# Residual sums of the post norms: from loaded tiles on VectorE and GpSimd to accumulating transfers into the scaled tile

## The chip, the cores and the metric

The kernel runs on one core of a Trainium2 chip. Its engines are named as in the profile: PE (TensorE, the matrix engine, with PEld for its weight loads), DVE (VectorE), ACT (ScalarE), POOL (GpSimd) and SP (SyncE, which here issues most transfers). Every engine works through its own list of instructions strictly in order, and engines wait for each other through semaphores. The metric is the device time of one execution in microseconds (us).

## The reference

One layer of a decoder over 1024 prompt tokens and 64 sample tokens (8 sequences of 8), model width 1024, all in fp32:

```
x = x + 1/2 * post1(SwiGLU_1(pre1(x)))          # FFN1, inner width 2816
h = pre_mix(x); z = h @ w_in + b_in
    A: sliding-window attention (window 128), 8 heads, 2 KV heads, sinks
    B: HGRN2 gated linear recurrence, chunkwise, 4 heads of 128 x 128
x = x + post_mix(concat(norm(attn), gate(hgrn)) @ w_out)
x = x + 1/2 * post2(SwiGLU_2(pre2(x)))          # FFN2

def rms_norm(x, g):
    y = x * rsqrt(mean(x * x, -1) + 1e-6)
    return y * g
```

So three times a branch's output y is multiplied by a factor per token (the inverse root) and a gain per feature, and added to the residual x. This sum, `x + scaled y`, is what the change touches. It is then both the input of the next norm and, stored to a buffer, the residual of the sum after it; after FFN2 it is the output.

## The kernel before

**Tiling.** The 1088 tokens form three thirds. Third 0 has 320 tokens (256 of the prompt and the 64 sample tokens) and is kept feature-major: a tile is 128 features by 320 tokens, eight of them make the width, and they lie in two `big` tiles of 128 x 4 x 384. Thirds 1 and 2 have 384 tokens each and are token-major where the norms run: two `big` tiles of 128 x 3 x 512, one for each half of the width (`hf`), with three blocks of 128 tokens (`i`). fp32 matmuls are made of three passes with operands split in a high and a low part (`mm3`, L260 to L262, after a cast on ACT, L240, and a subtraction on DVE, L241), so each weight tile must pass ACT and DVE before PE can use it. Thirds 1 and 2 share their FFN matmuls as seven products of sums and differences, the units p1 to p7 of `f.pair`.

**Stages.** FFN1 for third 0, then the units of thirds 1 and 2; w_in, mixer and w_out by thirds, mixed with the last units of FFN1 and the first of FFN2; FFN2; output. A norm runs as a *stream*: a generator that `stream(name, ...)` starts and that moves one `yield` further at certain points between groups of matmuls (`tick`), until `need(name)` runs it to its end. The streams give the program its order; a scheduler then lists the instructions of each engine from its own simulated timeline, so that the final order can differ from the program's.

**Post norms.** `post_t` (L335) is the feature-major form. After the broadcast of the inverse root, which `bcast_steps` makes from squares on ACT (L318, L321), it goes through the eight feature tiles: load 160 KB of the residual to a tile `xt` on SP (L346), scale the branch's tile by gain and root on DVE (L347), add `xt` on POOL (L349); at the end the sum is stored. It is used three times: after FFN1 (residual x0, stream c0), after the mixer (residual x1T, stream c0 again) and at the end (residual x2T, to the output of the sample and the first part of the prompt). `post_n` (L412) is the token-major form: for each of three blocks of tokens it loads two `xt` tiles of 256 KB (L416) and makes scale and sum in one DVE instruction (L428), six in all; where a destination `xdst` is given, each is stored at once (L430). It is used five times: after FFN1 for thirds 1 and 2 (streams c1, c2, residual in_x_rest), after the mixer for thirds 1 and 2 (residual x1N) and at the end for third 1 (residual x2N, stored to the output). Third 2's last sum has code of its own.

**What follows a post norm.** `pre_t`, `pre_n` and `pre_s` make the next norm of the sum. For thirds 1 and 2, `row_rms` takes squares on ACT (L383) and, behind each pair of squares, stores the sum as the next residual from ACT's queue (x1N, x2N, L388); after the root on DVE (L389 and on) both halves are scaled (L447/L449, L503) and PE transposes them (`tr`, L457, L513) for the following matmuls. `raw` is the staging tile of weight loads; L986 loads the differences of weights that FFN2's units use from a buffer `fb`.

Of the kernel before, what the change touches and what calls it, by code (L numbers as in the profile page):

```python
# [13 lines left out]
AF = mybir.ActivationFunctionType  # L14
ALU = mybir.AluOpType
# [3 lines left out]
P = 128  # L19
# [15 lines left out]
C_F1POST, C_MPRE, C_MPOST, C_F2PRE, C_F2POST, C_BIN, C_LB, C_HGN, C_AON = (  # L35
    0, 8, 16, 24, 32, 40, 62, 70, 71)
# [11 lines left out]
def tile_step(ctx: ExitStack, tc: tile.TileContext, A: dict, O: list):  # L48
    nc = tc.nc
    V, S, G, PE = nc.vector, nc.scalar, nc.gpsimd, nc.tensor  # L50
# [48 lines left out]
    def stream(name, gen, rate):  # L99
        streams[name] = [gen, rate, 0.0]  # L100
# [28 lines left out]
    cols = cp.tile([P, NROWS], F32, name="cols")  # L129
    f1pre = cp.tile([P, KC], F32, name="f1pre")  # L130
    halfpost = cp.tile([P, 16], F32, name="halfpost")
# [155 lines left out]
    def tmp2(name, shape=(P, 512)):  # L287
        return pp.tile(list(shape), F32, tag="t2", bufs=8, name=uid(name))
# [46 lines left out]
    def post_t(y, xsrc, gpost, xdst=None):  # L335

        w = WIDTH[0]

        def part(d):
            return y[d // 4][:, d % 4, :w]  # L340

        rb = []
        yield from bcast_steps(part, w, rb)
        for d in range(KC):
            xt = tmp2("xt")
            nc.sync.dma_start(xt[:, :w], xsrc(d))  # L346
            V.scalar_tensor_tensor(part(d), part(d), gpost[:, d:d + 1], rb[0],  # L347
                                   op0=ALU.mult, op1=ALU.mult)
            G.tensor_tensor(part(d), part(d), xt[:, :w], op=ALU.add)  # L349
            if d % 2:  # L350
                yield
        if xdst is not None:
            for hf in range(2):
                nc.sync.dma_start(xdst[:, 4 * hf:4 * hf + 4], y[hf][:, :, :w])

    def pre_t(y, gpre, h):
        w = WIDTH[0]

        def part(d):
            return y[d // 4][:, d % 4, :w]  # L360

        rb = []
        yield from bcast_steps(part, w, rb)
        h[0] = new_h(0)
        for d in range(KC):
            t = tmp2("ht")
            V.scalar_tensor_tensor(t[:, :w], part(d), gpre[:, d:d + 1], rb[0],
                                   op0=ALU.mult, op1=ALU.mult)
            hi, lo = hcol(h[0], d, w)
            split(hi, lo, t[:, :w], G)  # L370
            if d % 2:
                yield
# [37 lines left out]
            yield  # L410

    def post_n(n, y, sm, xsrc, xdst=None):  # L412
        def load(i):
            t = [tmp2("xt") for _ in range(2)]
            for hf in range(2):
                nc.sync.dma_start(t[hf], xsrc[i * P:(i + 1) * P, hf * 512:hf * 512 + 512])  # L416
            return t

        xt = load(0)
        V.scalar_tensor_tensor(sm[:, 0, 0:3], sm[:, 0, 0:3], EPS, sm[:, 0, 4:7], op0=ALU.add, op1=ALU.add)  # L420
        rsqrt(sm[:, 1, 0:3], sm[:, 0, 0:3], (sm[:, 2, 0:3], sm[:, 3, 0:3]))
        for i in range(3):
            if i:
                xt = load(i)
            for hf in range(2):
                cs = slice(hf * 512, hf * 512 + 512)
                t = y[hf][:, i]
                V.scalar_tensor_tensor(t, t, sm[:, 1, i:i + 1], xt[hf], op0=ALU.mult, op1=ALU.add)  # L428
                if xdst is not None:
                    nc.sync.dma_start(xdst[i * P:(i + 1) * P, cs], t)  # L430
            yield

    def pre_n(n, y, gpre, h, dst):

# [105 lines left out]
    x1T = dr.tile([P, KC, WIDTH[0]], F32, name="x1T")  # L540
    x2T = dr.tile([P, KC, WIDTH[0]], F32, name="x2T")
# [9 lines left out]
    def x0_part(d, n=1):  # L551
        return A["x0T"][:, d * WIDTH[0]:(d + n) * WIDTH[0]].rearrange("p (k t) -> p k t", k=n)
# [120 lines left out]
            wts.fill()  # L673
        return rb, banks

    def x0_all(d):
        return x0_part(d)[:, 0]

# [994 lines left out]
    def seq(*gens):  # L1675
        for g_ in gens:
            yield from g_

    RM = [0.88, 1.08, 1.24]
    RA0, RA1, RB0, RB1 = 1.2, 0.75, 0.6, 0.8  # L1680
# [15 lines left out]
    part = {}  # L1696
# [3 lines left out]
    hmix, hffn2 = {}, {}  # L1700
# [12 lines left out]
    def done1(n):  # L1713
        y, g = f1.ys[n], cols[:, C_MPRE:C_MPRE + 8]
        if n == 0:
            stream("c0", seq(post_t(y, x0_all, halfpost[:, 0:8], x1T), pre_t(y, g, hmix)), RA0)
        else:
            need("half")
            stream(f"c{n}", seq(half_n(y, 2 - n, sums[n], A["norm_ffn1_post"], 0.5),
                                post_n(n, y, sums[n], xN[n - 1]), pre_n(n, y, g, hmix, x1N[n - 1])), RA1)  # L1720
# [27 lines left out]
    part = {}  # L1748

    def done_mix(n):  # L1750
        y, g = ym[n], cols[:, C_F2PRE:C_F2PRE + 8]
        if n == 0:
            stream("c0", seq(post_t(y, lambda d: x1T[:, d], cols[:, C_MPOST:C_MPOST + 8], x2T), pre_t(y, g, hffn2)), RB0)
        else:
            stream(f"c{n}", seq(post_n(n, y, sums[n], x1N[n - 1]),
                                pre_s(n, y, g, part, f2.SF, x2N[n - 1])), RB1)
# [31 lines left out]
        w_out_units(2, ym, sums)  # L1788
        done_mix(2)
    def out0():  # L1790
        yield from post_t(f2.ys[0], lambda d: x2T[:, d], halfpost[:, 8:16], O[1])

    tail = {}

# [120 lines left out]
```

## Time and profile before

| | |
|---|---|
| time, median of 3 runs | 1937.84 us (1935.99 to 1938.87) |
| profiled execution: span from first to last instruction | 1937.4 us |
| PE busy | 1923.1 us (99%) |
| DVE / ACT / POOL busy | 1430.7 (74%) / 946.0 (49%) / 186.1 (10%) us |
| mean granted clock of PE | 0.999 |
| data moved by DMA | 375.56 MB, mean 194 GB/s |
| transfers on the queues q1 and q10 (kind: hardware_dynamic) | 169680 and 5904 packets, 56.0% and 1.5% of the engines' span |

The profile was taken from an execution of its own; its span is given, and the times of the three runs stand beside it. An engine that is busy for 74% of the span may be waiting for nothing and nobody may wait for it: what counts is which wait of PE it ends. In a group's row stand line, engine, operation, output<-input, count, and durations in ns (least/median/most). All transfers of this kernel are issued from SP or ACT; POOL issues none.

### The profile page before, as it was taken

How to read it: one execution, taken by the hardware profiler on the slowest of the kernel's cores; microseconds unless marked ns; L12 is line 12 of the kernel's file. 1: busy time of each engine (PE TensorE's matmuls, PEld its weight loads, DVE VectorE, ACT ScalarE, POOL GpSimd, SP SyncE). 2: the span in 40 equal slices, each digit the busy share in tenths (PEclk: the TensorE clock that was granted, in tenths of full speed). 3: DMA queues.
4: the chain of work that ended last, by engine and by line, in shares of the span. 5: the costliest groups of instructions: out<-in, count | busy, mean ns of one | idle time of the engine just before them, and what ended most of it. 6: DMA issues, size and time to landing. Idle time of an engine off the chain costs nothing.

```text
span 1937.4 us, 34843 instructions
## 1 busy us (share of the span) xinstructions
PE 1923.1 (99%) x13547; PEld 1806.1 (93%) x13547; DVE 1430.7 (74%) x2469; ACT 946.0 (49%) x1701; POOL 186.1 (10%) x227
## 2 busy tenths in 40 slices
PE   9999999999999999999999999999999999999998
PEld 9999999999998987788999888989999999999886
DVE  6896789877568666787678758756987887656666
ACT  5553444444455434545445545846544444445452
POOL 0300000000004022020221212000000000000102
PEclk9999999999999999999999999999999999999999
DMA  6643676555767556765334344546555555667974
GB/s 248 209 133 115 232 267 247 206 191 184 242 217 242 180 155 215 283 220 163 114 102 153 99 140 142 164 147 209 185 198 192 198 188 189 210 228 241 308 255 141
DMA packets 175750, 375.56 MB, mean 194 GB/s; under 512 B 16144, under 2 KB 67536, under 8 KB 175568
## 3 DMA queue, kind: packets, MB, share of 16 engines
q1 hardware_dynamic: 169680, 362.84, 56.0%
q10 hardware_dynamic: 5904, 10.49, 1.5%
q8 instruction: 106, 1.74, 0.4%
q14 instruction: 60, 0.49, 0.1%
HBM read 290.86 MB, written 83.39 MB: 193 GB/s over the span
## 4 chain that ended last, share of the span: by engine, by line
PE 88%; DMA 6%; DVE 3%; ACT 1%; issue 1%; POOL 1%; SPq 0%; ACTq 0%; DVEq 0%; POOLq 0%
PE mm L260 27%; PE mm L262 26%; PE mm L261 26%; DMA ar<-fa 1%; DMA xt<-in_x_rest_dram 1%; DMA ar<-act 1%; PE lv L1337 1%; PE sc L1237 1%; DMA raw<-in_ffn_w_gu_dram 1%; PE pv L1283 1%; DVE w L241 1%; PE pT L1269 1%; PE c L262 0%; PE c L260 0%; PE c L261 0%
## 5 line engine op out<-in xcount | busy, mean ns | idle before, releaser
L260 PE MATMUL mm<-h,wsph 128*128 128x320 f32 (+1 forms) x1344 | 427.2, 319 | 0.4 <-DVE big L814 0.4
L261 PE MATMUL mm<-h,wsph 128*128 128x320 f32 (+1 forms) x1344 | 425.5, 317 | 0.2 <-DVE h L241 0.2
L262 PE MATMUL mm<-h,wspl 128*128 128x320 f32 (+1 forms) x1344 | 422.6, 316 | 0.0
L241 DVE TENSOR_TENSOR wspl<-raw,wsph 128x1024 fp32r<-128x1024 f32 x208 | 260.8, 1255 | 125.2 <-ACT wsph L240 124.1
L240 ACT CAST wsph<-raw 128x1024 fp32r<-128x1024 f32 x208 | 217.8, 1049 | 254.0 <-PE mm L261 199.3
L260 PEld LDWEIGHTS mm<-h,wsph 128*128 128x128 f32 x1344 | 252.2, 188 | 4.2 <-issue 2.3
L261 PEld LDWEIGHTS mm<-h,wsph 128*128 128x128 f32 x1344 | 252.5, 188 | 3.9 <-issue 2.3
L262 PEld LDWEIGHTS mm<-h,wspl 128*128 128x128 f32 x1344 | 251.9, 188 | 3.4 <-issue 3.1
L240 ACT CAST w<-raw 128x512 fp32r<-128x512 f32 (+1 forms) x208 | 153.8, 745 | 199.9 <-PE mm L261 96.2
L261 PE MATMUL mm<-h,w 128*128 128x384 f32 (+1 forms) x736 | 245.6, 334 | 0.3 <-DVE h L622 0.3
L260 PE MATMUL mm<-h,w 128*128 128x384 f32 (+1 forms) x736 | 245.7, 334 | 0.2 <-ACT h L620 0.2
L262 PE MATMUL mm<-h,w 128*128 128x384 f32 (+1 forms) x736 | 239.6, 333 | 0.5 <-POOL w L613 0.4
L241 DVE TENSOR_TENSOR w<-raw,w 128x512 fp32r<-128x512 f32 (+1 forms) x208 | 178.3, 861 | 72.6 <-ACT w L240 71.7
L261 PE MATMUL mm<-w,h 128*128 128x512 f32 x462 | 180.5, 391 | 0.7 <-DVE w L241 0.7
L260 PE MATMUL mm<-w,h 128*128 128x512 f32 x462 | 180.8, 394 | 0.0
L262 PE MATMUL mm<-w,h 128*128 128x512 f32 x462 | 179.8, 391 | 0.0
L260 PE MATMUL mm<-big,w 128*128 128x384 f32 x528 | 176.7, 335 | 0.3 <-ACT big L806 0.2
L261 PE MATMUL mm<-big,w 128*128 128x384 f32 x528 | 176.5, 334 | 0.0
L262 PE MATMUL mm<-big,w 128*128 128x384 f32 x528 | 176.0, 334 | 0.0
L261 PEld LDWEIGHTS mm<-h,w 128*128 128x128 f32 x736 | 138.1, 188 | 1.1 <-DVE h L622 0.8
L260 PEld LDWEIGHTS mm<-h,w 128*128 128x128 f32 x736 | 138.1, 188 | 0.8 <-ACT h L620 0.5
L262 PEld LDWEIGHTS mm<-h,w 128*128 128x128 f32 x736 | 137.6, 188 | 1.0 <-POOL w L613 0.7
(367 smaller groups left out, 3353.8 us busy)
## 6 DMA issues: line engine op xcount, KB each, us to landing
raw<-in_ffn_w_gu_dram SPq DMA_DIRECT2D x162, 512.0 KB
raw<-in_ffn_w_down_dram SPq DMA_DIRECT2D x74, 512.0 KB
raw<-in_w_in_dram SPq DMA_DIRECT2D x54, 512.0 KB
ar<-fa SPq DMA_DIRECT2D x70, 384.0 KB
big<-in_ffn_w_down_dram SPq DMA_DIRECT2D x88, 256.0 KB
fb<-big SPq DMA_DIRECT2D x44, 512.0 KB
fa<-big SPq DMA_DIRECT2D x22, 768.0 KB
raw<-fb SPq DMA_DIRECT2D x30, 512.0 KB
```

Source lines behind the costliest of these rows:

```text
L240: made['S'] = S.copy(hi, src).ins
L241: (lo_eng or V).tensor_tensor(lo, src, hi.bitcast(F32), op=ALU.subtract)
L260: PE.matmul(out, a[0], b[0], start=first, stop=False, skip_group_check=resume)
L261: PE.matmul(out, a[0], b[1], start=False, stop=False, skip_group_check=resume)
L262: return PE.matmul(out, a[1], b[0], start=False, stop=last, skip_group_check=resume).ins
L1237: PE.matmul(banks[g][rows(hq), i, cs], zq[rows(g), 2 * pr + i, b * P + 64 * hq:b * P + 64 * hq + 64], kx[rows(g), k0 + cs.start:k0 + cs.st ...
L1269: PE.transpose(tb2[hq][:, g, i, slot], pt[g][rows(hq), c:c + P], ident[rows(hq), rows(hq)])
L1283: PE.matmul(ob[par][rows(g), :, hq], vn[rows(par), b + (blk + hq) // 2, rows(g)], pT[hq][rows(par), g, :, PLACE[hq][blk]], start=alone or ...
L1337: PE.matmul(b5[32 * i:32 * i + 32, b, a], K[:, a, cs], Q[:, a, cs], start=True, stop=True)
```

## The change

In `post_t` the loaded tile and POOL's addition are gone. DVE scales as before; behind each second feature tile GpSimd issues a transfer that reads two feature tiles of the residual (128 x 2 x 320, 320 KB) from memory and adds them to the scaled tile in place (`accum_op=ALU.add`): four for each use. One `yield` more follows.

In `post_n` the loads and the six DVE instructions are gone. The first half of the width (`hf` 0) is scaled by three DVE instructions, the second by three of ACT, and behind each half GpSimd issues one accumulating transfer of 768 KB (128 x 3 x 512). The store to `xdst`, where there is one, is one of 768 KB for each half instead of three of 256 KB. The work goes half by half instead of block by block, and yields stand after the root, after each half and at the end.

In all 24 additions on POOL, 30 sums on DVE and 54 loads on SP go, and 15 scalings on DVE, 15 on ACT and 22 accumulating transfers on POOL's queue come: 12 of 320 KB and 10 of 768 KB. The lines behind the change are numbered 3 lower than before.

```diff
@@ -342,13 +342,13 @@
         rb = []
         yield from bcast_steps(part, w, rb)
         for d in range(KC):
-            xt = tmp2("xt")
-            nc.sync.dma_start(xt[:, :w], xsrc(d))
             V.scalar_tensor_tensor(part(d), part(d), gpost[:, d:d + 1], rb[0],
                                    op0=ALU.mult, op1=ALU.mult)
-            G.tensor_tensor(part(d), part(d), xt[:, :w], op=ALU.add)
+            if d % 2:
+                nc.gpsimd.dma_start(y[d // 4][:, d % 4 - 1:d % 4 + 1, :w], xsrc(d - 1), accum_op=ALU.add)
             if d % 2:
                 yield
+        yield
         if xdst is not None:
             for hf in range(2):
                 nc.sync.dma_start(xdst[:, 4 * hf:4 * hf + 4], y[hf][:, :, :w])
@@ -410,25 +410,22 @@
             yield
 
     def post_n(n, y, sm, xsrc, xdst=None):
-        def load(i):
-            t = [tmp2("xt") for _ in range(2)]
-            for hf in range(2):
-                nc.sync.dma_start(t[hf], xsrc[i * P:(i + 1) * P, hf * 512:hf * 512 + 512])
-            return t
-
-        xt = load(0)
         V.scalar_tensor_tensor(sm[:, 0, 0:3], sm[:, 0, 0:3], EPS, sm[:, 0, 4:7], op0=ALU.add, op1=ALU.add)
         rsqrt(sm[:, 1, 0:3], sm[:, 0, 0:3], (sm[:, 2, 0:3], sm[:, 3, 0:3]))
-        for i in range(3):
-            if i:
-                xt = load(i)
-            for hf in range(2):
-                cs = slice(hf * 512, hf * 512 + 512)
+        yield
+        for hf in range(2):
+            cs = slice(hf * 512, hf * 512 + 512)
+            for i in range(3):
                 t = y[hf][:, i]
-                V.scalar_tensor_tensor(t, t, sm[:, 1, i:i + 1], xt[hf], op0=ALU.mult, op1=ALU.add)
-                if xdst is not None:
-                    nc.sync.dma_start(xdst[i * P:(i + 1) * P, cs], t)
-            yield
+                if hf:
+                    S.activation(t, t, AF.Copy, scale=sm[:, 1, i:i + 1])
+                else:
+                    V.tensor_scalar(t, t, sm[:, 1, i:i + 1], None, op0=ALU.mult)
+            nc.gpsimd.dma_start(y[hf], xsrc[0:384, cs].rearrange("(i p) c -> p i c", p=P), accum_op=ALU.add)
+            yield
+            if xdst is not None:
+                nc.sync.dma_start(xdst[0:384, cs].rearrange("(i p) c -> p i c", p=P), y[hf])
+        yield
 
     def pre_n(n, y, gpre, h, dst):
 
@@ -673,8 +670,8 @@
             wts.fill()
         return rb, banks
 
-    def x0_all(d):
-        return x0_part(d)[:, 0]
+    def x0_two(d):
+        return x0_part(d, 2)
 
 
 
@@ -1713,7 +1710,7 @@
     def done1(n):
         y, g = f1.ys[n], cols[:, C_MPRE:C_MPRE + 8]
         if n == 0:
-            stream("c0", seq(post_t(y, x0_all, halfpost[:, 0:8], x1T), pre_t(y, g, hmix)), RA0)
+            stream("c0", seq(post_t(y, x0_two, halfpost[:, 0:8], x1T), pre_t(y, g, hmix)), RA0)
         else:
             need("half")
             stream(f"c{n}", seq(half_n(y, 2 - n, sums[n], A["norm_ffn1_post"], 0.5),
@@ -1750,7 +1747,7 @@
     def done_mix(n):
         y, g = ym[n], cols[:, C_F2PRE:C_F2PRE + 8]
         if n == 0:
-            stream("c0", seq(post_t(y, lambda d: x1T[:, d], cols[:, C_MPOST:C_MPOST + 8], x2T), pre_t(y, g, hffn2)), RB0)
+            stream("c0", seq(post_t(y, lambda d: x1T[:, d:d + 2], cols[:, C_MPOST:C_MPOST + 8], x2T), pre_t(y, g, hffn2)), RB0)
         else:
             stream(f"c{n}", seq(post_n(n, y, sums[n], x1N[n - 1]),
                                 pre_s(n, y, g, part, f2.SF, x2N[n - 1])), RB1)
@@ -1788,7 +1785,7 @@
         w_out_units(2, ym, sums)
         done_mix(2)
     def out0():
-        yield from post_t(f2.ys[0], lambda d: x2T[:, d], halfpost[:, 8:16], O[1])
+        yield from post_t(f2.ys[0], lambda d: x2T[:, d:d + 2], halfpost[:, 8:16], O[1])
 
     tail = {}
 
```

The scheduler makes a new order from this. Three places are shown as they stand in the lists of the engines, with the name of a tile and its number, and x2 or x3 for repeats.

The first is ACT's list around the squares of the sum of third 1 after FFN1 (big_5802 and big_6080 are the two halves before, big_5802 and big_6047 after; `h_`/`ar_` are activations of FFN units, `t_117x`/`t_116x` scores of the attention). Before:

```order
L240 CAST h_8305<-ar_8306 128x2x384
L240 CAST h_8390<-ar_8391 128x2x384
L383 ACTIVATE junk,sm_8268<-big_5802 128x512
L1255 ACTIVATE t_1173_8114,sm_8102<-t_1173_8114,sm_8101 128x192 x2
L1255 ACTIVATE t_1174_8119,sm_8102<-t_1174_8119,sm_8101 128x192 x2
L383 ACTIVATE junk,sm_8268<-big_6080 128x512
L388 DMA x1N_98<-big_5802 128x512
L1259 ACTIVATE sm_8101<-sm_8101 128x2x2
```

After:

```order
L240 CAST h_8275<-ar_8276 128x2x384
L421 ACTIVATE big_6047<-big_6047,sm_7145 128x512 x3
L240 CAST h_8360<-ar_8361 128x2x384
L1252 ACTIVATE t_1165_8094,sm_8082<-t_1165_8094,sm_8081 128x192 x2
L1252 ACTIVATE t_1166_8099,sm_8082<-t_1166_8099,sm_8081 128x192 x2
L1256 ACTIVATE sm_8081<-sm_8081 128x2x2
L383 ACTIVATE junk,sm_8245<-big_5802 128x512
L240 CAST h_8414<-ar_8415 128x2x384
L383 ACTIVATE junk,sm_8245<-big_6047 128x512
```

The three scalings of the second half are new ahead of the exponentials, and all squares now stand behind the exponentials.

The second is ACT's list around the same place after the mixer (third 1, halves big_12166 and big_12167 before, big_12106 and big_12107 after; `wsph` are weights of FFN2's third 0, `sg` its silu). Before:

```order
L716 COPY sg_13162<-mm_13078 128x320
L719 ACTIVATE sg_13162<-sg_13162 128x320
L240 CAST wsph_13327<-raw_13325 128x1024
L383 ACTIVATE junk,sm_13128<-big_12166 128x512
L1196 CAST h_12209<-t_1895_13202 128x4x128
L383 ACTIVATE junk,sm_13128<-big_12167 128x512
L388 DMA x2N_100<-big_12166 128x512
L388 DMA x2N_100<-big_12167 128x512
L1255 ACT_TABLE_LOAD
L1255 ACTIVATE t_1887_13111,sm_13099<-t_1887_13111,sm_13098 128x192 x2
```

After:

```order
L716 ACTIVATE sg_13070<-sg_13070 128x320
L1252 ACT_TABLE_LOAD
L1252 ACTIVATE t_1853_13041,sm_13029<-t_1853_13041,sm_13028 128x192 x2
L1252 ACTIVATE t_1854_13046,sm_13029<-t_1854_13046,sm_13028 128x192
L421 ACTIVATE big_12107<-big_12107,sm_12108 128x512 x3
L1252 ACTIVATE t_1854_13046,sm_13029<-t_1854_13046,sm_13028 128x192
L1256 ACTIVATE sm_13028<-sm_13028 128x2x2
L240 CAST wsph_13142<-raw_13140 128x1024
L1193 CAST h_12149<-t_1861_13130 128x4x128
L240 CAST wsph_13251<-raw_13249 128x1024
L383 ACTIVATE junk,sm_13091<-big_12106 128x512
```

The table load and the exponentials moved ahead of the scalings of the second half, and two weight casts stand between these and the first square.

The third is the end of SP's list (the stores of third 1's output among the last loads of weights of FFN2). Before:

```order
L986 DMA raw_20022<-fb_6444 128x2x512
L986 DMA raw_20056<-fb_6444 128x2x512
L430 DMA out_dram<-big_18892 128x512
L430 DMA out_dram<-big_19134 128x512
...
L430 DMA out_dram<-big_19134 128x512
L986 DMA raw_20097<-fb_6444 128x2x512
L986 DMA raw_20127<-fb_6444 128x2x512
L986 DMA raw_20144<-fb_6444 128x512
L1827 DMA out_dram<-yg_20178 128x512
```

After:

```order
L983 DMA raw_19942<-fb_6424 128x2x512
L983 DMA raw_19983<-fb_6424 128x2x512
L427 DMA out_dram<-big_18812 128x3x512
L983 DMA raw_20013<-fb_6424 128x2x512
L427 DMA out_dram<-big_19034 128x3x512
L983 DMA raw_20030<-fb_6424 128x512
L1824 DMA out_dram<-yg_20064 128x512
```

Each of the two larger stores waits for its accumulating transfer; one weight load stands between them and one behind them, where three stood behind all stores before.

## The prediction

> **What bounds the kernel now.** I read the page's busy shares and slices first, then the waits of TensorE, then one tile (the loaded residual, xt), and last the timelines around each post norm.
>
> ```profile
> span 1937.4 us, 34843 instructions
> PE 1923.1 (99%) x13547; PEld 1806.1 (93%) x13547; DVE 1430.7 (74%) x2469; ACT 946.0 (49%) x1701; POOL 186.1 (10%) x227
> PE   9999999999999999999999999999999999999998
> ```
> TensorE (PE) works 1923.1 of 1937.4 us, in every slice: it idles 14.3 us in all. So less work on VectorE (DVE), GpSimd (POOL) or the load queue (SP) shortens nothing by itself; a gain can only come out of those 14.3 us, and any lateness that reaches PE is added whole. The waits of PE (us in total, times, longest), summed by releaser, say how much of the idle time hangs on the residuals:
>
> ```profile
> PE spT L1517 <- ACT t L1512: 1.3, 1, 1.3
> PE av L1454 <- ACT t L1292: 1.1, 1, 1.1
> PE mm L261 <- DVE w L241: 0.7, 1, 0.7
> ```
> All three releasers stand on their engine behind an instruction that waits for the residual sum; the timelines below show each. Together 3.1 us: the whole visible prize.
>
> ```profile
> L428 DVE SCALAR_TENSOR_TENSOR big<-big,sm,xt x30: 743/747/1777, 786.4 to 1900.8; 128x512 f32<-128x512 f32 x30
> L349 POOL TENSOR_TENSOR big<-big,xt x24: 860/881/1857, 583.0 to 1797.2; 128x320 f32<-128x320 f32 x24
>   ACT junk L383: 19.8, 5
> ```
> These are the instructions that go (operation, count, least/median/most ns), and the engine that already waits for them: ScalarE (ACT), whose squares L383 waited 19.8 us in 5 places.
>
> **The change part by part.** *Work removed and added.* DVE loses 30 x 0.747 = 22.4 us; half comes back as 15 scalings on DVE, half as 15 on ACT. Their prices are those of the same forms elsewhere in the kernel:
>
> ```profile
> L449 DVE TENSOR_SCALAR big<-big,sm x6: 475/482/487, 810.4 to 879.6; 128x512 f32<-128x512 f32 x6
> L447 ACT ACTIVATE big<-big,sm x6: 711/711/724, 811.1 to 880.0; 128x512 f32<-128x512 f32 x6
> ```
> That is 7.2 us on DVE and 10.7 on ACT. POOL loses 24 x 0.881 = 21.1 us; SP loses 54 issues of loads. All of it lies beside PE's matmuls and is worth nothing to the end. What matters is the delay from the scaled tile to the finished sum: 0.75 us on DVE before, one accumulating transfer now.
>
> *The price of that transfer* has no row: the kernel has no accumulating DMA. The nearest rows, from the chain of waits, are a 768 KB load, a 768 KB store and one 256 KB residual load, with the issues of the latter on SP:
>
> ```profile
> 39.02 6.29 DMA big<-in_xT_dram
> 274.33 9.12 DMA fa<-big
> 868.28 4.58 DMA xt<-in_x_rest_dram
> L416 SPq DMA_DIRECT2D xt<-in_x_rest_dram x12: 327/365/1450, 771.6 to 868.3; - x12
> ```
> Nothing smaller than 4.58 us bounds it below. From above I take reading the tile and writing it back in series, 6.29 + 9.12 = 15.4. I choose the load's 6.29 for each 768 KB half, since bytes and direction are those of the load, with the two halves behind each other and 1 us of issue (an issue on SP takes 0.33 to 1.45 us in the last row): 1 + 2 x 6.29 = 13.6, about 14 us from the first scaled half to both sums. Issued 1 us apart and side by side it would be 8.3; at the upper end, 1 + 2 x 15.4, 31.8.
>
> By the Trainium skill's "DMA: Bandwidth & Descriptors" (Anatomy of one DMA) a GpSimd-issued transfer takes 2.0 us + bytes/436 GB/s, an estimate of 3.8 us for 768 KB; the load row above, 6.29 under this kernel's traffic, disagrees, and the row decides. By the page's figure the pair would take 8.6 us and the sum would be near rival 1.
>
> *Feature-major third after FFN1 (c0).* The rows are of the timelines: start, busy us, instruction, and in brackets the idle time before it and who ended it.
>
> ```profile
> 582.97 9.96 POOL L349 TENSOR_TENSOR big<-big,xt 128x320 f32<-128x320 f32 x8 [109.70 <-DMA xt<-in_x0T_dram]
> 580.40 3.75 DVE L347 SCALAR_TENSOR_TENSOR big<-big,halfpost,rb 128x320 f32<-128x320 f32 x8
> 589.60 1.03 ACT L240 CAST w<-raw 128x1024 fp32r<-128x1024 f32 x1
> 592.25 0.50 PE L261 MATMUL mm<-w,h 128*128 128x512 f32 x1 [0.74 <-DVE w L241]
> ```
> The weight cast at 589.60 stands behind squares of the sum, and PE waited 0.74 us for it. Now four squares precede it, so it needs the second 320 KB piece: scaled by 582.3 (4 of the 8 scalings), issued by 583.3, and with a price between 4.58 and 6.29 there at 587.9 to 589.6. I take 589.1; two squares of 0.47 put the cast at 590.05: +0.5 (below: the stall goes, -0.7; above: pieces at 15.4/6.29 = 2.4 times the price, +9).
>
> *Third 1 after FFN1 (c1).*
> ```profile
> 786.39 2.08 DVE L428 SCALAR_TENSOR_TENSOR big<-big,sm,xt 128x512 f32<-128x512 f32 x3
> 807.10 0.63 ACT L383 ACTIVATE junk<-big 128x512 bf16<-128x512 f32 x1 [2.52 <-DVE big L428]
> 807.64 0.19 ACT L383 ACTIVATION_READ_ACCUMULATOR junk<-big 128x1 f32 x1
> 810.22 0.35 ACT L1292 COPY t<-pv 128x256 f32<-128x256 f32 x1
> 810.63 0.49 PE L1454 MATMUL av<-big,big 128*128 128x128 f32 x2 [1.10 <-ACT t L1292]
> ```
> Before, the last residual load was late, ACT's square at 807.10 waited, and the copy for PE behind it. Now the scalings end near 788 and both halves are there at 802. From the first square on the second half to that copy ACT has eight squares in its order (0.63 and 0.19 to read the sum: 6.6 us), two casts and two copies (0.6 to 0.8 each, 2.6) and a scaling of 0.71, 9.9 in all: copy at 811.9, against 810.2. Value +1.6; below, with both halves there at 796, -1.1 (the stall goes); above +19.
>
> *Third 2 (c2).*
> ```profile
> 872.88 1.78 DVE L428 SCALAR_TENSOR_TENSOR big<-big,sm,xt 128x512 f32<-128x512 f32 x1 [0.53 <-DMA xt<-in_x_rest_dram]
> 875.77 0.41 ACT L1512 ACTIVATE t<-t,sm 128x136 f32<-128x136 f32 x1
> 876.32 0.33 PE L1517 MATMUL spT<-ident,t 128*128 128x128 f32 x1 [1.33 <-ACT t L1512]
> ```
> Scaled from 855.4 on, the sum is there at 871.4, before the late load let DVE finish (874.7): the 1.3 us go, -1.3; above +15.
>
> *After the mixer.* For thirds 0 and 2 the transposes or the broadcast that follow stand later in PE's changed order than before, so that the longer way is covered:
>
> ```profile
> 1321.14 2.74 DVE L428 SCALAR_TENSOR_TENSOR big<-big,sm,xt 128x512 f32<-128x512 f32 x4
> 1336.42 0.38 PE L513 MATMUL tr<-ident,big 128*128 128x128 f32 x2
> ```
> In third 2 the first scaled half is there at 1322, both sums at 1336, six squares and the root (6 x 0.82 + 1.8) later it is 1342.7; the transposes stand 7.2 us of matmuls later, at 1343.6. +0.5 for the casts of weights behind those squares (0; +18), and 0 for third 0 (0; +2). Third 1 has no such cover:
>
> ```profile
> 1201.40 4.07 DVE L428 SCALAR_TENSOR_TENSOR big<-big,sm,xt 128x512 f32<-128x512 f32 x6
> 1203.44 0.47 ACT L719 ACTIVATE sg<-sg 128x320 f32<-128x320 f32 x1
> 1208.83 1.28 ACT L1255 ACT_TABLE_LOAD   x1
> 1218.10 0.16 DVE L389 SCALAR_TENSOR_TENSOR sm<-sm 128x3 f32<-128x3 f32 x1
> 1220.13 1.27 DVE L503 TENSOR_SCALAR big<-big,sm 128x512 f32<-128x512 f32 x3
> L513 PE MATMUL tr<-ident,big x48: 270/272/273, 1222.4 to 1351.1; 128*128 128x128 f32 x48
> ```
> PE transposes the normed tile from 1222.4, about 2 us behind the scaling. In the changed order these transposes stand 2.7 us of matmuls earlier, so at 1219.7. ACT, in its changed order, after the silu (1203.9) loads a table (1.28), makes three exponentials (about 0.45 each, once DVE has their maxima, which I put at 1205.5) and only then the scalings of half 1, to 1208.9; its transfer is issued to 1209.9 and lands at 1216.2. Behind it ACT still has the squares (four of 0.8), a weight cast (1.05), two copies, a second table load and a silu: 7.6 us, to 1223.8; the root takes 1.8 (1218.10 to 1219.83) and a scaling 0.5: 1226, or +6. With 4.58 us and without the second table load it is +3; above, 15.4 for each half, +24.
>
> *Out of the last mile.* The sample third's output sum is stored, and no matmul reads it (0; +5). The last third 1 shares SP with the last weights of FFN2:
>
> ```profile
> 1897.49 4.06 DVE L428 SCALAR_TENSOR_TENSOR big<-big,sm,xt 128x512 f32<-128x512 f32 x6
> 1902.72 6.00 SPq L986 DMA_DIRECT2D raw<-fb  x3
> 1916.07 2.46 DVE L241 TENSOR_TENSOR w<-raw,w 128x1024 fp32r<-128x1024 f32 x2 [0.46 <-ACT w L240]
> 1920.89 0.69 DVE L1011 TENSOR_TENSOR big<-mm,big 128x512 f32<-128x512 f32 x1 [2.36 <-PE mm L262]
> ```
> SP now waits, for the sums, in front of two stores, and the last weight load stands behind the second store. Scaled by 1899.6, the second half is there at 1913.2; SP issues store and load by 1914.3; the load lands between 1918.9 (4.58) and 1923.4 (behind the store's 9.12). With 1.3 us of cast and split the weight is ready at 1920.2 to 1924.7, where 2.36 us of slack end at about 1920.2: 0 to +4.5, value +3.5; above +18.
>
> Sum: 0.5 + 1.6 - 1.3 + 0 + 6 + 0.5 + 0 + 3.5 = +10.8 on the span, 1948.2; the median of the runs, 1937.84, is 0.4 above the span, so **1948.6 us**. All lower ends: -0.7 - 1.1 - 1.3 + 3 = -0.1. All upper ends: 9 + 19 + 15 + 2 + 24 + 18 + 5 + 18 = +110.
>
> **Rivals.** *1, no change (1937.3 to 1941.7):* the transfers land no later than plain loads, side by side, and the three stalls pay for the mixer's third 1: -0.1 on the span. For it: PE has 99% cover at nearly all places. Against it: the software queue shares the DMA engines with weight loads, and ACT's order is in-line. A difference under 0.2% (3.9 us) cannot be told from no change.
>
> *2, faster (about 1933):* the sums are there before ACT comes to them. Its place is the mixer's third 1: half 1 would have to be there by 1210.0 (1219.7 less 7.6, 1.8 and 0.5), where its last scaling alone ends at 1208.9. Then nothing is added, the 3.1 us go, 1934.7 beside the median, and 2 more would have to come out of the other 11 us of idle time, with DVE's 15 us less work. For it speaks only that ACT's order ahead of the scalings may run sooner than I put it, once DVE hands over its exponentials sooner.
>
> *3, much slower (1980 to 2040):* the price is nearer read plus write back, or issue is held up. Places on ACT and SP where casts stand behind a waiting square then cost 9 to 24 us each; half of the upper ends is +55, 1992. As a mechanism of issue, if GpSimd prepared its transfers only while DVE rests:
>
> ```profile
> 780.00:800.00 20.00, 20.00 (x124) 16.17 (x123) 16.06 (x43) 8.72 (x23) 2.14 (x2) 1.00 0.96 336
> ```
> DVE (the third busy time, behind PE and its weight loads) works 16.06 of 20 us there, so 1 us of issue becomes 5.1: +8.2 for a pair, +41 over five places, 1990 with the forecast's sum. Against it: every kind of DVE instruction would have to hold GpSimd up. The Trainium skill's "SBUF — State Buffer" says so for two-port DVE instructions such as tensor_scalar only, which lock GpSimd out of writing descriptors (620 ns became 3100 ns); no row here can show it, as no DMA is issued by GpSimd.
>
> *4, that the change does not do what it says:* the order shows 22 accumulating transfers directly on the scaled tiles and no loaded residual; excluded.
>
> **How the numbers follow.** Forecast 0.56 (1942 to 1980), rival 1 0.24, rival 2 0.06, rival 3 0.14. So faster 0.06, same 0.24, slower 0.70. The range 1935 to 1980 leaves out rival 2, the lowest sliver of rival 1 and most of rival 3; its upper end is +42, four tenths of all upper ends.
>
> **What would show it.** Right: ACT's squares L383 wait for the accumulating transfers, no longer for DVE; PE idles before the first transposes after the mixer's third 1 (about 6 us) and before the last weights (about 3.5), and the 1.3 us before spT are gone. Wrong: a 768 KB accumulate that lands within 5 us or takes over 10; PE idle in the c0 or c1 places of more than 2 us; PE idle still 14 us in all.

## The result and the profile after

The changed kernel takes 1998.76 us (median of 4 runs, 1996.23 to 2001.85) against 1937.5 us for the kernel before on the same chip: a ratio of 1.0317, 95% interval 1.0305 to 1.0329, 61 us slower. The forecast was 1948.6 (1935 to 1980): the sign was right, the size was not. The page of the kernel after, first lines and the new queue:

```profile
span 2000.1 us, 34729 instructions
PE 1947.2 (97%) x13547; PEld 1819.2 (91%) x13547; DVE 1414.6 (71%) x2454; ACT 958.7 (48%) x1718; POOL 188.0 (9%) x225
q0 software_dynamic: 7264, 11.80, 3.8%
```

DVE does 16 us less work, as forecast, and it does not matter. The span grew by 62.7 us, in two parts that the second line gives. PE idles 2000.1 - 1947.2 = 52.9 us instead of 14.3: **+38.6**. And the same 13547 matmuls keep it busy for 1947.2 instead of 1923.1 us: **+24.1**. The second part was in no term of the prediction. (The profile models the ends of matmuls, so its busy time is not work at full speed.)

The idle part, by the waits of PE (us in total, times, longest):

```profile
PE mm L260 <- ACT w L240: 10.0, 3, 5.5
PE pv L1280 <- DVE t L1271: 8.7, 2, 8.2
PE av L1451 <- ACT t L1289: 7.4, 1, 7.4
PE spT L1514 <- ACT t L1509: 2.8, 1, 2.8
```

Before, the longest wait in this view was 1.3. And by place, in windows of 10 us around the post norms (length, busy us and count of PE, PEld, DVE, ACT, POOL, then the granted clock, which is the share of its full clock that PE was given, the DMA share and GB/s):

```profile
590.00:600.00 10.00, 3.24 (x9) 1.54 (x8) 2.99 (x4) 2.61 (x5) 1.21 (x1) 0.74 0.81 202
600.00:610.00 10.00, 8.76 (x30) 7.09 (x31) 6.24 (x8) 6.94 (x12) 1.22 (x1) 0.74 0.66 170
810.00:820.00 10.00, 4.08 (x17) 2.93 (x16) 1.76 (x3) 0.18 (x1) 2.54 (x2) 1.00 1.07 297
820.00:830.00 10.00, 6.67 (x58) 5.18 (x59) 5.69 (x20) 9.12 (x23) 1.79 (x5) 0.66 0.70 242
1240.00:1250.00 10.00, 5.38 (x66) 4.62 (x64) 0.00 (x0) 2.40 (x6) 1.87 (x5) 1.00 0.70 159
1250.00:1260.00 10.00, 7.21 (x39) 7.21 (x40) 6.34 (x27) 9.76 (x27) 0.00 (x0) 0.66 0.68 228
1380.00:1390.00 10.00, 6.07 (x36) 5.34 (x36) 5.42 (x16) 8.36 (x19) 0.00 (x0) 0.84 0.72 247
1860.00:1870.00 10.00, 4.48 (x21) 3.40 (x19) 0.17 (x1) 0.82 (x2) 0.75 (x1) 0.90 0.71 186
1970.00:1980.00 10.00, 7.89 (x33) 5.58 (x31) 6.06 (x3) 1.86 (x4) 3.66 (x3) 1.00 0.79 210
```

And the window of the first place in the kernel before:

```profile
590.00:600.00 10.00, 9.26 (x41) 7.32 (x40) 9.26 (x12) 8.40 (x14) 2.93 (x3) 1.00 1.03 355
```

Each place shows idle time of PE, and at or right behind it a granted clock under 1.00 (behind the last one, 0.83 from 1980 to 1990). In the kernel before the clock is 1.00 in all such windows but the last, 1930 to the end, where PE idles 7.10 us and the clock is 0.74. Matmuls that run at such a clock take longer, and that is most of the second part: in the trace's record of the clock, stretches of 3.4 to 10.2 us at 0.50 take 17.8 of the 24.1 us out of PE's busy time. Where the other 6 come from is not shown.

Where the waits come from is seen on GpSimd. After FFN1, third 0 (c0), and then third 1 (c1), the timeline of POOL:

```profile
581.12 1.38 POOL L348 DMA_DIRECT2D big<-in_x0T_dram  x1 [107.75 <-DVE big L345]
586.44 1.24 POOL L348 DMA_DIRECT2D big<-in_x0T_dram  x1 [3.95 <-DVE h L241]
591.46 1.21 POOL L348 DMA_DIRECT2D big<-in_x0T_dram  x1 [3.77 <-issue]
600.13 1.22 POOL L348 DMA_DIRECT2D big<-in_x0T_dram  x1 [7.46 <-issue]
...
798.77 1.30 POOL L424 DMA_DIRECT2D big<-in_x_rest_dram  x1 [19.93 <-DVE big L423]
807.84 1.30 POOL L424 DMA_DIRECT2D big<-in_x_rest_dram  x1 [7.77 <-issue]
```

DVE had scaled all of c0's tiles by 583.6, and the program's own waits of the later transfers are only for scaled tiles and older work. Still they are issued 5.3, 5.0 and 8.7 us apart. ScalarE shows why these times: its squares are released by the landings, at 586.26, 591.28 and 599.89, each 0.2 us before the next issue. One accumulating transfer is under way at a time. ACT in c0 and c1, and PE behind it:

```profile
599.89 0.83 ACT L321 ACTIVATE sq<-big 128x320 f32<-128x320 f32 x2 [6.11 <-DMA big<-in_x0T_dram]
600.63 1.05 ACT L1011 COPY big<-mm 128x512 f32<-128x512 f32 x2
819.82 0.63 ACT L383 ACTIVATE junk<-big 128x512 bf16<-128x512 f32 x1 [10.85 <-DMA big<-in_x_rest_dram]
```
```profile
601.25 0.80 PE L260 MATMUL mm<-w,h 128*128 128x512 f32 x1 [4.82 <-ACT big L1011]
823.33 1.56 PE L1280 MATMUL pv<-t,vn 64*64 64x128 f32 x24 [8.18 <-DVE t L1271]
```

The copy that empties a matmul bank (L1011) and a copy of the transposed scores (L1271) stand on ScalarE behind a square that waits for a landing. (The profile names DVE for the second wait: DVE makes the other half of that copy, and had itself waited 9.62 us for a cast of ScalarE behind the same square.) A pair of 768 KB takes 819.82 - 798.77 = 21 us here instead of the 14 assumed.

At the end it is SyncE. Its timeline around the stores of the sample third's output:

```profile
1840.42 0.36 SPq L995 DMA_DIRECT2D ar<-fa  x1
1850.46 0.38 SPq L354 DMA_DIRECT2D out_dram<-big  x1
...
1864.48 0.38 SPq L354 DMA_DIRECT2D out_dram<-big  x1
1864.95 0.46 SPq L983 DMA_DIRECT2D raw<-fb  x1
```

Both stores wait for their accumulating transfers, SyncE issues nothing for 9.7 and some 12 us, and the weight loads (raw) behind them are late: PE waited 5.5 us for the cast of one.

### The profile page after: what moved, and what is told of

The parts are those of the page before. It is cut to its first block, busy times and chain, and to the rows that moved or that the text cites. A ratio compares the mean times of both kernels' runs of the same rounds, so it can differ in the third digit from the quotient of the medians.

```text
span 2000.1 us, 34729 instructions
## 1 busy us (share of the span) xinstructions
PE 1947.2 (97%) x13547; PEld 1819.2 (91%) x13547; DVE 1414.6 (71%) x2454; ACT 958.7 (48%) x1718; POOL 188.0 (9%) x225
## 3 DMA queue, kind: packets, MB, share of 16 engines
q0 software_dynamic: 7264, 11.80, 3.8%
## 4 chain that ended last, share of the span: by engine, by line
PE 76%; issue 8%; DMA 8%; DVE 5%; ACT 2%; POOL 1%; SPq 0%; ACTq 0%; DVEq 0%; POOLq 0%
PE mm L260 23%; PE mm L262 23%; PE mm L261 23%; DMA big<-in_x_rest_dram 1%; DMA raw<-in_ffn_w_gu_dram 1%; DMA big<-x1N 1%; DVE w L241 1%; PE sc L1234 1%; DMA ar<-act 1%; PE lv L1334 1%; PE pv L1280 1%; DMA big<-x2N 1%; DVE wspl L241 0%; DMA raw<-fb 0%; DVE t L757 0%
## 5 line engine op out<-in xcount | busy, mean ns | idle before, releaser
L260 PE MATMUL mm<-w,h 128*128 128x512 f32 x462 | 184.0, 402 | 15.9 <-ACT w L240 10.0
L261 PE MATMUL mm<-w,h 128*128 128x512 f32 x462 | 183.8, 398 | 1.7 <-DVE w L241 1.7
L262 PE MATMUL mm<-w,h 128*128 128x512 f32 x462 | 181.9, 395 | 0.0
```

Source lines behind the costliest of these rows:

```text
L260: PE.matmul(out, a[0], b[0], start=first, stop=False, skip_group_check=resume)
L261: PE.matmul(out, a[0], b[1], start=False, stop=False, skip_group_check=resume)
L262: return PE.matmul(out, a[1], b[0], start=False, stop=last, skip_group_check=resume).ins
```

## The experiments

**Theory after the first look.** Three things add up: accumulating transfers go one at a time; what stands behind a waiting square on ScalarE, or behind a waiting store on SyncE, makes PE idle; and the longer idle stretches are followed by matmuls at half clock. Rivals: the new order of the whole program costs the time; the bytes of the transfers do; and, for the slower matmuls, contention with the transfers.

### One form at a time

The feature-major form alone (the token-major function as before):

```
 def post_n(...):           # as in the kernel before: loads of xt, one DVE instruction
 def post_t(...):           # as in the change: accumulating transfers
```

> Only the feature-major form (three uses, 320 KB transfers) is changed; the token-major form is as before. Theory: the accumulating transfers of one use go one behind another, each issued only when the one before has landed, so four take 20 to 24 us instead of the 9 I forecast; behind them stand, in order, ScalarE's weight casts (after FFN1) and SyncE's weight loads (behind the stores, after FFN1 and at the end), and each idle stretch of TensorE is followed by 3.4 to 10.2 us at half clock. By the trace of the changed kernel these places cost 7.3 us of idle time and 5.1 of clock after FFN1, 0.8 after the mixer, 5.8 and 3.4 at the end: +22, 1960. Rival (order): the loss comes from the new order of the whole program, not from the transfers; then the parts do not add up, and this alone may cost anything from 0 to 60. Rival (bytes): the loss goes with the bytes on the DMA engines; 3.9 of 11.8 MB, +20.

Measured 1959.9, ratio 1.0117 (1.0100 to 1.0134) to 1936.9: +23.1. The token-major form alone is the reverse edit:

> Only the token-major form (five uses, 768 KB transfers) is changed. Theory: two serial transfers of 8 to 12 us each in front of ScalarE's squares; by the trace of the changed kernel idle time and half clock of about 11.5 us after FFN1 for third 1, 7 for third 2, 11 and 7 after the mixer, 4.5 at the end: +41, 1979, and with the other part alone it adds up to the whole loss of 61 within 5. Rival (order): no such sum. Rival (bytes): +41 too, so this run alone does not tell bytes from theory.

Measured 1979.8, ratio 1.0223 (1.0207 to 1.0238): +42.9. The parts add to 66.0, where both together cost 61.3, about as the places in the trace say. An order that costs time by itself would have no reason to fall apart in this way, though this does not exclude it; bytes and theory are not told apart yet.

### The same transfers without the addition

```
-  nc.gpsimd.dma_start(y[hf], xsrc[...], accum_op=ALU.add)
+  nc.gpsimd.dma_start(y[hf], xsrc[...])             # in both forms
```

> The changed kernel with the same transfers on the same queue at the same places, but as plain copies: the residual overwrites the scaled tile instead of being added to it (so the sums of branch and residual are left out). Theory (queue): one transfer at a time is the way of this software queue as it is set up here, whatever it does with the bytes; issues stay 5 to 9 us apart for 320 KB and 8 to 9 for 768 KB, time 1990 to 2000. Rival (accumulation): the addition at the target makes the transfer slow or exclusive; then plain ones overlap, the second is issued some 1.3 us behind the first, a pair lands in 9 us and the time is under 1965.

This kernel leaves out the sums, so it serves for its time alone. Measured 1940.5, ratio 1.0016 (1.0006 to 1.0025). My theory, that this queue takes one transfer at a time whatever it does with the bytes, fell; the rival, that the addition makes the transfers exclusive or slow, holds. The queue's line on the page, its token-major landings, and c1 on POOL:

```profile
q0 software_dynamic: 3040, 11.80, 1.9%
DMA to landing us min/median/max: 5.3/6.9/9.3
786.34 1.55 POOL L424 DMA_DIRECT2D big<-in_x_rest_dram  x2 [19.21 <-DVE big L423]
```

Here both halves are issued back to back in 1.55 us. The same 11.80 MB take 3040 packets and 1.9% of the DMA engines' span, against 7264 and 3.8% with the addition. The list of every engine in this kernel is that of the change, row for row, so order, larger stores, moved scalings and the plain transfers themselves together cost the 3.7 us by which it is slower than the kernel before (1.2 to 4.8 by the interval).

### A larger descriptor ring

A setting of the program gives the queue of GpSimd its descriptor space (the ring, where the entries that describe a transfer wait), 1024 bytes of each partition here. For 3072, one scratch tile t2 makes room: 512 numbers of 4 bytes are 2048 bytes of each partition.

```
-  tag="t2", bufs=8                     +  tag="t2", bufs=7
-  dynamic_dma_scratch_size=1024        +  dynamic_dma_scratch_size=3072
```

> The changed kernel with three times the descriptor space of the software queue (3072 instead of 1024 bytes of each partition; for it, the pool of scratch tiles t2, which no longer holds loaded residuals, has 7 tiles instead of 8). Theory with the ring as the reason of the one-at-a-time issue: the second transfer of a pair is issued 1.3 us behind the first, pairs land in 9 to 12 us instead of 17 to 20, and the time falls by 20 us or more, under 1980. Theory with one-at-a-time as a property of the queue: 1999 within 4 and the same spacing. Rival (bytes): 1999 as well, but the transfers would overlap.

Measured 1967.8, ratio 1.0166 (1.0148 to 1.0184). Control, the seven tiles without the ring:

> Control for the run with the larger ring: the changed kernel with 7 instead of 8 scratch tiles t2 and the ring as it was (1024 bytes). If the 31 us that the larger ring gave back came from the overlap of the transfers, this is 1999 within 4, with issues one behind another; if they came from the other number of tiles (another order), it is near 1968.

Measured 2002.9 (ratio 1.0328, 1.0308 to 1.0348). So it is the ring: 35 us with the lists of all engines the same, 31 against the change itself. c1 on POOL and the token-major landings with the larger ring, its span and engines; then c1 of the control:

```profile
787.47 2.62 POOL L424 DMA_DIRECT2D big<-in_x_rest_dram  x2 [19.32 <-DVE big L423]
DMA to landing us min/median/max: 7.2/9.9/13.9
span 1964.6 us, 34771 instructions
PE 1936.7 (99%) x13547; PEld 1815.8 (92%) x13547; DVE 1404.9 (72%) x2454; ACT 959.2 (49%) x1718; POOL 191.1 (10%) x225
```
```profile
797.73 1.30 POOL L424 DMA_DIRECT2D big<-in_x_rest_dram  x1 [19.22 <-DVE big L423]
806.06 1.30 POOL L424 DMA_DIRECT2D big<-in_x_rest_dram  x1 [7.03 <-issue]
```

With the ring, a pair is issued in 2.6 us and overlaps, and each transfer lands after 9.9 us in the median (7.2 to 13.9, from the start of its issue), plain ones after 6.9. So the 61 us divide in three, about: the ring 31 (1998.8 to 1967.8; 35 against the control), the addition with a ring of 3072 bytes 27 (1967.8 to 1940.5; no run tries a larger one), the rest 3.7. The ring run is also what I had priced: its five pairs land 13.8 to 14.7 us after their first issue, and I had put 13.6. It idles 1964.6 - 1936.7 = 27.9 us, 13.6 more than before, where the prediction's terms summed to 10.8; and PE is busy 13.6 us longer, which they did not have (9.6 of it by the record of the clock).

### Who stands behind a late sum: SyncE

On the feature-major kernel (1959.9), the stores of the sums go to GpSimd's queue:

```
-                nc.sync.dma_start(xdst[:, 4 * hf:4 * hf + 4], y[hf][:, :, :w])
+                nc.gpsimd.dma_start(xdst[:, 4 * hf:4 * hf + 4], y[hf][:, :, :w])
```

> Only the feature-major form is changed (the kernel of 1959.9), and its six stores of the sums are issued from GpSimd instead of SyncE. Theory: at the end the 5.2 us of idle time and 3.4 us of clock come from weight loads that stand on SyncE behind stores which wait for the accumulating transfers; with the stores elsewhere they go, 1951, and SyncE issues weight loads through. After FFN1 the wait is that of ScalarE's order and stays (8 us idle). Rival (ScalarE everywhere, or transfers that slow the weight loads down): 1959 within 3.

Measured 1958.8 (ratio 1.0108, 1.0092 to 1.0124), not 1951. The end went as the theory says, but another place opened. The end with the stores on SyncE, then on GpSimd, and the place after the mixer in the latter; then its longest wait of PE and GpSimd's list there:

```profile
1820.00:1840.00 20.00, 14.80 (x63) 11.61 (x62) 4.39 (x5) 3.48 (x5) 1.22 (x1) 0.92 0.83 236
```
```profile
1820.00:1840.00 20.00, 20.00 (x90) 16.57 (x89) 11.13 (x13) 9.99 (x12) 2.42 (x2) 1.00 1.03 293
1040.00:1060.00 20.00, 11.74 (x73) 11.15 (x72) 8.85 (x23) 4.89 (x13) 3.39 (x7) 0.83 0.54 135
```
```profile
PE pT L1269 <- POOL t L1244: 8.3, 1, 8.3
1049.91 0.81 POOL L354 DMA_DIRECT2D x2T<-big  x1 [5.52 <-DMA big<-x1T]
1053.96 0.78 POOL L354 DMA_DIRECT2D x2T<-big  x1 [3.24 <-issue]
1054.78 0.14 POOL L1243 MEMSET t<- 64x64 f32 x1
```

PE's 5.2 us of idle time at the end are gone. After the mixer GpSimd now waits in front of the stores, four small fills that attention needs stand behind them, and PE idles 8.3 us. The stall moved to the queue that took the waiting store.

The same with the larger ring and all stores of the sums:

> The larger ring (and 7 tiles t2), and all stores of the sums of the post norms issued from GpSimd instead of SyncE. Theory: with the ring the transfers overlap and what is left, 13.6 us of idle time and 13.6 us of slower matmuls, is nearly all behind ScalarE's squares; the last place alone (1.8 idle, 1.7 of clock) can be SyncE's: 1963 to 1968. Rival (SyncE's queue is the bound): under 1955.

Measured 1977.7 (ratio 1.0206, 1.0187 to 1.0224): 10 us worse than the ring alone. Moving the stores gains nothing here. That the stores now share the one software queue with the additions, or that they hold up GpSimd's list as in the run before, may be the reason; no run separates them, so what SyncE's line costs the ring kernel stays open.

### Who stands behind a late sum: ScalarE

More yields at the end of each post norm let the scheduler put the squares later on ScalarE:

```
-        yield
+        for _ in range(12):      # 6 in the run with the larger ring
+            yield
```

> The changed kernel with eleven more yields at the end of each post norm, so that the squares of the sum stand some 25 instructions later on ScalarE, behind weight casts and copies that have nothing to do with the sum. Theory (ScalarE's order): where other work stood behind waiting squares (after FFN1 for all thirds, third 1 after the mixer) the waits of TensorE for casts and copies shrink by 15 us of idle time or more, and the clock's share with them: 1965 to 1980. Rival (TensorE waits for the sum itself): the stalls only change their names, to waits for transposes and the mean's matmul, 1995 or more.

Measured 2007.5 (ratio 1.0380, 1.0346 to 1.0415): no gain, and a time in the rival's range. The longest of PE's waits, a new one:

```profile
PE tr L456 <- ACT junk L405: 10.2, 1, 10.2
```

The first transposes of the normed tile now wait, but not for the sum: it had landed at 818.7, and its squares begin only at 841.6, behind other work of ScalarE. So the edit put the squares too late, and the run decides neither for the theory nor for the rival; the squares have to come early as well as the sum.

> The larger ring with 7 tiles t2 (1967.8), and five more yields at the end of each post norm. Theory (ScalarE's order): with transfers that overlap (12 us for a pair) and squares that stand later, most of the remaining 13.6 us of idle time goes: 1940 to 1955. Rival (the sum itself is waited for): 1968 within 5, with waits at transposes.

Measured 1961.1 (ratio 1.0118, 1.0102 to 1.0135), 6.7 less than the ring alone and above the range of the theory: some of the remaining time is ScalarE's order. How much of the rest is stays open, since the new order brings a wait of 5.6 us of its own (a weight cast at 1392, held up by DVE).

### What an idle stretch costs by itself

The kernel before, without any accumulating transfer, with six weight tiles that pass through a chain of copies on the idle GpSimd:

```
+  LATE = {3: 6, 6: 8, 9: 10, 12: 12, 15: 14, 18: 16}      # unit: number of copies
+            if tag == 2 and m == 1 and u in LATE:
+                dl = tmp2("dl")
+                G.tensor_copy(dl, src)
+                for _ in range(LATE[u] - 1):
+                    G.tensor_copy(dl, dl)
+                src = dl
```

> The kernel before, in which six weight tiles of FFN2's up-projection pass through chains of 6, 8, 10, 12, 14 and 16 copies on the idle GpSimd before they are split, some 60 us apart: TensorE is made to wait with no accumulating transfer anywhere. Theory (clock): the longer of these stalls are each followed by one or more stretches of 3.4 us at half clock and cost that much more than their idle time (a stretch of 3.4 us costs 1.7); stalls under 2 us cost their idle time alone. Rival (the slower matmuls of the changed kernel come from contention with the transfers): idle time only, clock 1.00 all the way.

Measured 1938.8, ratio 1.0004 (0.9994 to 1.0015): inconclusive, since all chains were hidden. With 18 to 28 copies:

> As the run with late weights, whose chains of 6 to 16 copies were all hidden (0.57 us of idle time behind the longest): now 18, 20, 22, 24, 26 and 28 copies of 0.95 us, so stalls of TensorE of about 2 to 11 us, far from any accumulating transfer. Theory (clock): the stalls from about 4 us on are each followed by 3.4 to 10.2 us at half clock, and the time grows by the idle time plus half of those stretches: with 35 us idle and five stretches of 6.8, 35 + 17 = 52, near 1990. Rival (contention makes matmuls slower, not idleness): clock 1.00 behind every stall, 35 alone, near 1972.

Measured 1983.8, ratio 1.0239 (1.0217 to 1.0261): +46. The page, and windows of 4 us around one of the stalls:

```profile
span 1982.6 us, 34985 instructions
PE 1938.6 (98%) x13547; PEld 1815.4 (92%) x13547; DVE 1469.9 (74%) x2469; ACT 943.6 (48%) x1701; POOL 317.2 (16%) x365
```
```profile
1478.00:1482.00 4.00, 0.54 (x2) 0.54 (x3) 4.00 (x8) 2.03 (x4) 0.00 (x0) 0.81 0.35 97
1482.00:1486.00 4.00, 4.00 (x14) 4.00 (x13) 3.32 (x5) 1.71 (x4) 1.32 (x2) 0.50 0.96 350
1486.00:1490.00 4.00, 4.00 (x21) 4.00 (x21) 3.97 (x5) 0.70 (x2) 3.75 (x5) 0.84 0.90 281
```

PE idles 44.0 us, 29.7 more than before, and is busy 15.5 us longer for the same matmuls. Behind the idle time the clock is at 0.50 and back at full soon after: the shortfall of 0.19, 0.50 and 0.16 over 4 us each is 3.4 us, so 6.8 us at half rate. So idle time slows the matmuls behind it without any transfer that accumulates, and contention is not needed for it. By the record of the clock this is 10.7 of the 15.5 us here, as it is 17.8 of 24.1 in the changed kernel; that contention has a part in the rest, 5 to 6 us in each, is neither shown nor excluded. The Trainium skill's "TensorE: Matmul & The Clock Gate" (Part 1: The HAM clock gate) says that an idle window of about 3.4 us halves the clock until a busy one has passed, and the stretch here is twice that length.

### The opposite cure

Instead of accumulating, the kernel before with two blocks of the residual loaded ahead:

```
-        xt = load(0)
+        xts = [load(0), load(1)]
...
-            if i:
-                xt = load(i)
+            xt = xts.pop(0)
+            if i == 0:
+                xts.append(load(2))
```

> The kernel before, with the loads of the second and third block of the residual issued one block sooner on SyncE (nothing accumulates): the opposite cure for the 1.1 and 1.3 us that TensorE waited behind late residual loads after FFN1. Theory: these 2.4 us go, 1935 against 1937.5, at the edge of what can be told (ratio 0.9987). Rival: the loads were late for want of free scratch tiles, and the time stays.

Measured 1939.0, ratio 1.0010 (1.0001 to 1.0019): not faster. The wait for spT shrank from 1.3 to 0.7 us and the one for av is gone, and a new one took their place:

```profile
PE mm L260 <- ACT big L1669: 1.6, 1, 1.6
```

No version here beats the kernel before.

## Why the prediction was right in sign and wrong in size

**Right.** PE bounds the kernel and its idle time is the only prize: 16 us less of DVE's work gained nothing. The losses are where squares on ScalarE and stores on SyncE wait for the accumulating transfers. The price of one transfer was bounded well: 4.58 to 15.4 us were the ends, 7.2 to 12.1 was measured for 768 KB, with 8.6 in the middle where I took 6.29 (and 1 us of issue once for a pair; the 8.6 has the 1.3 us of its own issue in it).

**Wrong, first step: "with the two halves behind each other and 1 us of issue".** I let the second half be queued at once and wait only for the engines, 1 + 2 x 6.29. It was not issued before the first had landed, so each half pays its 1.3 us of issue and its whole way, 16 to 21 us for a pair, and four pieces of c0 took until about 605. The ring runs show this as a setting of this kernel, and it is half of the loss: with 3072 bytes the pairs take the 14 us that I had put. Between "behind each other" and "side by side", my sum had no case for a queue that holds one transfer.

**Wrong, second step: "any lateness that reaches PE is added whole".** It is added more than whole. Idle time of 38.6 us brought 24.1 us of slower matmuls with it, 29.7 us brought 15.5 in the run without transfers, and in the ring run 13.6 brought as much again, though no wait there is longer than 5.0 us. At its post norms the kernel before has stalls of at most 1.3 us and shows nothing of this; but my own forecast had stalls of 3.5 and 6 us, and the last window of before, with 7.10 us idle and a clock of 0.74, could have warned me. The rule of the Trainium skill's page named above (TensorE: Matmul & The Clock Gate) speaks against the change at exactly this point. I did not weigh either.

**By place**, idle time of PE against the terms (as change from before; from the windows and waits above):

| place | forecast | measured idle | |
|---|---|---|---|
| third 0 after FFN1 (c0) | +0.5 | +7.3 (8.0 less 0.74) | first cast followed only; the bank copies behind the third piece's squares left out |
| third 1 after FFN1 | +1.6 | +8.1 (9.25 less 1.1) | pair of 21 us |
| third 2 after FFN1 | -1.3 | +1.5 (2.8 less 1.3) | stall not removed but doubled |
| third 1 after the mixer | +6 | +7.4 | place right, mechanism wrong: the size is luck |
| third 2 after the mixer | +0.5 | +3.9 | cover used up by the serial pair |
| sample third at the end | 0 | +5.5 | step failed: "no matmul reads it" |
| last third 1 | +3.5 | +2.1 | place and mechanism right |

The fourth row came out near its number by luck. The forecast had PE wait for the first transposes of the normed tile, at the end of squares, root and scaling. The trace has no wait there:

```profile
1249.29 0.63 ACT L383 ACTIVATE junk<-big 128x512 bf16<-128x512 f32 x1 [7.42 <-DMA big<-x1N]
1252.80 0.80 PE L1451 MATMUL av<-big,big 128*128 128x128 f32 x2 [7.42 <-ACT t L1289]
1260.21 0.27 PE L510 MATMUL tr<-ident,big 128*128 128x128 f32 x1
```

PE waited earlier, at a matmul of the attention (`av`), for a copy that stands on ScalarE behind the square of the second half: the mechanism that I had used for c1 and did not look for here.

The sixth row is an error of reading, not of price. I looked for who reads the sum, and nobody does; but SyncE reads it to store it, and weight loads stand behind the store. I had used that very mechanism for the last row and did not apply it one row higher.

**The rivals.** The time lies in rival 3's stretch (1980 to 2040, given 0.14), and its first sentence, a price nearer read plus write back or held-up issue, is half right: issue was held up, the price is not near 15.4. Its mechanism is not right: in the changed kernel GpSimd's issue of a transfer takes 1.2 to 1.4 us in all places, also at 581.12, where DVE worked without a pause, and at 1043.85, beside a TENSOR_SCALAR of DVE (1.23), so DVE does not hold it up. That also leaves no sign here of the lock for which I cited the Trainium skill's "SBUF — State Buffer". By the Trainium skill's "DMA: Bandwidth & Descriptors" (Anatomy of one DMA), an estimate for a 768 KB transfer is 3.8 us. Plain ones from GpSimd took 6.9 in the median under this traffic, so rival 1 could not rest on that figure either. But had the transfers cost what the plain ones do, rival 1 would have been right: 1940.5.

## What to carry to other kernels

A transfer that takes over an engine's addition is cheap only if nobody stands in line behind its result: list, for each engine and queue that waits for it (stores too), what comes next in that list. Price a stall of the matrix engine above its idle time once it lasts several microseconds: the added idle time here came out at 1.4 times itself (the run with the squares too late: 48.4 idle, 19.9 of slower matmuls) to 2 times (the ring run). Before using GpSimd's queue for several transfers in flight, look at how many its descriptor space holds, since a program without such transfers may have cut it down for the sake of its buffers.

## What the hardware showed that I had not expected

In this kernel an accumulating transfer costs the DMA engines twice what a plain copy of the same bytes does: 7264 packets and 3.8% of the engines' span against 3040 and 1.9%, for 11.80 MB; its issue takes 1.28 us against 0.77 (768 KB), its landing in the median 9.9 us against 6.9 with two under way. And 1024 bytes of descriptor space let one accumulating transfer of 320 or 768 KB be under way at a time, but two plain ones of 768 KB; with 3072 bytes four accumulating ones of 320 KB were issued before the first had landed (580.27 to 585.37, landing at 585.51).
